# Streaming encoder step: a larger DMA count per gathered row in the planner, and fewer pauses in the row-tile normalization

## The chip, the cores and the metric

The kernel runs on one core of a Trainium2 chip. The metric is the device time of one execution in microseconds (us), from launch to end; lower is better. The engines named below are TensorE (PE, with its weight loads PEld), VectorE (DVE), ScalarE (ACT), GpSimd (POOL) and SyncE (SP), and the 16 DMA engines that all queues of the core share.

## What is computed

One layer of a hybrid encoder over 1024 prompt rows and 64 sample rows of width 1024: window attention and retention, an output projection and layer norm, then a mixture of 16,384 single-row experts (PEER) and a last layer norm. The step concerned is the mixture:

```python
def block(xb):                       # rows of the stream, after the first layer norm
    q = einsum('td,de->te', xb, wq).reshape(PEER_BLOCK, PEER_HEADS, 2, PEER_DK_HALF)
    s = einsum('tpcd,pcnd->tpcn', q, sub_keys)
    s1, i1 = top_k(s[:, :, 0], 16);  s2, i2 = top_k(s[:, :, 1], 16)
    # the best 16 of the 256 pairs, for each of 8 heads: 128 experts for each row
    top_s, sel = top_k(cand_s, 16);  eidx = take_along_axis(cand_i, sel, axis=-1)
    g = softmax(top_s)
    act = gelu(einsum('tpkd,td->tpk', u_tab[eidx], xb))
    return einsum('tpk,tpkd->td', g * act, v_tab[eidx])
h <- LN2(ALPHA * h + peer(h))
```

## The kernel before

The nine row tiles (eight of 128 prompt rows, one with the 64 sample rows, `TS`) go two ways through the mixture. Five tiles (`DENSE`, 640 rows) are **dense**: all 16,384 experts are multiplied with all rows, and a table `G` of gate weights, zero where an expert was not chosen, selects. The other four tiles are **gathered**: for each chosen expert its row of `u` and of `v` is fetched from DRAM by index. Both run at the same time, in what is called the dense stretch here.

**Dense work.** The experts are 128 blocks of 128. For block i, `u_mm` (L1352) multiplies the block's `u` with the 640 rows (48 matmuls into PSUM tile `pA`: high and low halves of the operands in three products), ACT applies the gelu, and DVE multiplies with the gate table (`ge<-pA,gt`, one such instruction for each block, so that it counts blocks). `v_mm` (L1392) multiplies the result with the block's `v`, for three blocks together: 10 units of 9 matmuls (`y`), each followed on DVE by an add into the sum in SBUF (`Y<-y,Y`). Three blocks with their 10 units are called a triple below. For each block SP issues loads of `u` (`ur<-ut`, 512 KB), of `v` (`vr<-vt`, twice 256 KB), and for each second block of five pieces of the gate table (`gt<-G`, 128 KB each); POOL makes the low halves (`ul`, `vl`, `wl`).

**Gathered work.** It comes in 448 slots, 64 for the sample tile (whose second half lies on partitions 64 to 127) and 128 for each of the tiles 5, 6 and 7. A slot needs one gather on POOL's queue (L239: 128 rows of `u` and `v` together, 8 KB each, into one of four buffers `uv`), then on DVE `uv<-uv,ph` (the dot product with the row), on ACT the gelu and gate (`gav`), and on DVE `pacc<-uv,gav,pacc` (the weighted add into PSUM tile `pacc`), which frees the buffer. Up to three gathers are issued ahead of their slot (`LEAD`).

**What sets the order.** Each engine runs its instructions in the order in which the program writes them. The dense units are written one by one, and after each of them `pump` (L392) decides whether slots are written next. It goes by a planner, `est`: counts of the time that each engine and the DMA have been given so far. For each gather `issue` (L232) adds a count to the planner's DMA time (L243) and from it notes when the data should be there (`avail`); `pump` writes no slot whose `avail` lies ahead of the planner's present time (the later of PE's and DVE's counts). So a larger count puts the slots farther apart among the dense units. The planner does not know what the chip does; it only sets an order.

**End of a gathered tile.** After its last slot the sum is copied to `gacc`, and `finish` (L271) normalizes it. For the first three of the four tiles the norm's weights `ln2_g` and `ln2_b` are loaded into one of the four `uv` buffers (`lnx`), so that three are left for gathers until the norm has read them. For the sample tile its second half is moved down to partitions 0 to 63 and added first. `finish` and `norm_out` (L289) are generators: each `yield` lets one further slot be written before the next step.

Of the kernel before, what the change touches and what calls it, by code (L numbers as in the profile page):

```python
# [135 lines left out]
def hymba_peer_step(ctx, tc, a, o):  # L136
    nc0 = tc.nc
    est = Est()
# [14 lines left out]
    def rows_bcast(ap, n):  # L153
        return bass.AP(tensor=ap.tensor, offset=ap.offset, ap=[[0, 128], [1, n]])
# [51 lines left out]
    def halves(t):  # L206
        return [t[:, 0:512], t[:, 512:1024]]
# [7 lines left out]
    def open_tile(t):  # L215
        d = spill[t]
        h1 = gat.tile([128, D], F32, name="gh1")
        g = gat.tile([128, 128], F32, name="gg", bufs=2)
        idx = gat.tile([128, 128], I32, name="gi", bufs=2)
        if t == TS:  # L220
            for i, (lo, hi) in enumerate(((0, NS), (NS, 128))):
                nc.sync.dma_start(h1[lo:hi], d["h1"])
                nc.sync.dma_start(g[lo:hi, 0:64], d["g"][:, i * 64:(i + 1) * 64])
                nc.sync.dma_start(idx[lo:hi, 0:64], d["idx"][:, i * 64:(i + 1) * 64])
        else:
            nc.sync.dma_start(idx, d["idx"])
            nc.sync.dma_start(h1, d["h1"])
            nc.sync.dma_start(g, d["g"])
        av = gat.tile([128, 128], F32, name="gav", bufs=2)
        tl[t] = dict(h1=h1, g=g, idx=idx, av=av, left=64 if t == TS else 128)  # L230

    def issue():  # L232
        k = ctl["issued"]
        t, j = slots[k]
        if t not in tl:
            open_tile(t)
        R = ctl["uvp"].tile([128, 2 * D], F32, name="uv", tag="uv")
        rows_uv[k] = R
        nc0.gpsimd.indirect_dma_start(out=R, out_offset=None, in_=a["uv"],  # L239
                                      in_offset=bass.IndirectOffsetOnAxis(ap=tl[t]["idx"][:, j:j + 1], axis=0))  # L240
        est.t["pool"] += 1.04
        ctl["pq"] = max(ctl["pq"], now()) + GTC
        est.t["dma"] = max(est.t["dma"], max(est.t["pe"], est.t["dve"]) - 3.0) + 2.6  # L243
        ctl["avail"][k] = max(est.t["dma"] + 2.0, max(ctl["pq"], now()) + ctl["slack"])
        ctl["issued"] = k + 1

# [10 lines left out]
    def accum(k):  # L257
        t, j = slots[k]
        d = tl[t]
        acc = banked(t, d, "acc")  # L260
        nc.vector.scalar_tensor_tensor(acc, rows_uv[k][:, D:2 * D], d["av"][:, j:j + 1], acc,
                                       op0=OP.mult, op1=OP.add)
        del rows_uv[k]
        ctl["done"] = k
        d["left"] -= 1
        if d["left"] == 0:
            d["acc"] = gat.tile([128, D], F32, name="gacc")
            nc.scalar.activation(d["acc"], acc, AF.Copy)
            ctl["fin"].append(finish(t, d))

    def finish(t, d):  # L271
        r, q = d["acc"], 128
        ln2, late = ctl["ln2"], t == TS
        if ln2 is None or t == TS:
            x = ctl["uvp"].tile([128, 2 * D], F32, name="lnx", tag="uv")
            ln2 = [x[:, 0:D], x[:, D:2 * D]]
            nc.sync.dma_start(ln2[0], rows_bcast(a["ln2_g"], D))
            if t == TS:
                q = NS
                nc.sync.dma_start(ln2[1][0:NS], r[NS:128])  # L280
                yield
                yield
                yield
                yield
                nc.vector.tensor_tensor(r[0:NS], r[0:NS], ln2[1][0:NS], op=OP.add)
            nc.sync.dma_start(ln2[1], rows_bcast(a["ln2_b"], D))
        yield from norm_out(gat, t, r, q, ln2)

    def norm_out(pool, t, r, q, ln2, st=None):  # L289
        wide = st is not None  # L290
        if not wide:
            st = pool.tile([128, 2, 6], F32, name="stf", bufs=2)
            for i, x in enumerate(halves(r)):
                nc.vector.bn_stats(st[:q, i], x[:q])
        mv = pool.tile([128, 3], F32, name="mvf", bufs=2)
        nc.vector.bn_aggr(mv[:q, 0:2], st[:q])
        nc.vector.tensor_scalar(mv[:q, 1:2], mv[:q, 1:2], EPS, None, op0=OP.add)
        nc.gpsimd.tensor_tensor(mv[:q, 2:3], mv[:q, 1:2], epsc[:q, 0:1], op=OP.pow)
        if wide:
            nc.gpsimd.tensor_tensor(mv[:q, 0:1], mv[:q, 0:1], mv[:q, 2:3], op=OP.mult)  # L300
            nc.gpsimd.tensor_scalar(mv[:q, 0:1], mv[:q, 0:1], -1.0, None, op0=OP.mult)
            yield
            nc.scalar.activation(r[:q], r[:q], AF.Identity, bias=mv[:q, 0:1], scale=mv[:q, 2:3])
            yield
            nc.gpsimd.tensor_tensor(r[:q], r[:q], ln2[0][:q], op=OP.mult)
            yield
            eng = nc.gpsimd if DENSE.index(t) in PAD else nc.vector
            eng.tensor_tensor(r[:q], r[:q], ln2[1][:q], op=OP.add)
            nc.sync.dma_start(o["y_p"][t * 128:(t + 1) * 128, :], r)
            return  # L310
        for _ in range(4):
            yield
        nc.vector.scalar_tensor_tensor(r[:q], r[:q], mv[:q, 0:1], ln2[0][:q], op0=OP.subtract, op1=OP.mult)
        yield
        nc.vector.scalar_tensor_tensor(r[:q], r[:q], mv[:q, 2:3], ln2[1][:q], op0=OP.mult, op1=OP.add)
        if t == TS:
            nc.sync.dma_start(o["y_s"], r[:q])
        else:
            nc.sync.dma_start(o["y_p"][t * 128:(t + 1) * 128, :], r)
# [5 lines left out]
    def prefetch():  # L325
        if ctl["uvp"] is None:
            return
        while (ctl["issued"] < len(slots) and ctl["issued"] < ctl["k"] + ctl["lead"]
               and ready[slots[ctl["issued"]][0]]):
            issue()  # L330
# [30 lines left out]
    def now():  # L361
        return max(est.t["pe"], est.t["dve"])
# [875 lines left out]
    def dense(hx):  # L1238
# [206 lines left out]
        for n, (kind, i) in enumerate(ops):  # L1445
            last = kind == "v" and i[0] == NG - 1
            ctl["most"] = 4
            if n == SL[1]:
                ctl["slack"] = SL[2]
            if 2 <= n < 2 + NT:  # L1450
                nc.sync.dma_start(Y[:, n - 2], spill[DENSE[n - 2]]["h1"])
            if kind == "u":
                if i % 2 == 0:
                    g_load(i // 2 + 1)
                yield from u_mm(i)
            else:
                yield from v_mm(*i)
                if n == len(ops) - 2 * NT - 1:
                    ctl["ln2"] = [vp.tile([128, NT * 256], F32, name="ln2r", tag="gt", bufs=2)[:, 0:D] for _ in range(2)]
                    for x, k in zip(ctl["ln2"], ("ln2_g", "ln2_b")):  # L1460
                        nc.sync.dma_start(x, rows_bcast(a[k], D))
            if last:
                if can_slot():
                    slot()
                for g in outs:
                    next(g, None)
                if i[1]:
                    outs.append(norm_out(xp, DENSE[i[2]], Y[:, i[2]], 128, ctl["ln2"], yst[i[2]]))
            yield
# [136 lines left out]
```

## Time and profile before

| what | value |
|---|---|
| median of 3 runs | 3320.02 us (3319.77 to 3331.34) |
| the profiled execution, its own time | 3355.53 us |
| span of that execution, first to last instruction | 3353.8 us |
| dense stretch while gathers run (1291.9 to 3140.3 us) | 1848.4 us, 113 blocks, 447 slots |
| rest of the dense blocks (3140.3 to 3297.7 us) | 157.4 us, 11 blocks, no slot but the last one's end |
| from there to the end of the span | 56.1 us |

Times in the rows count from the first instruction. The profile is one execution; DMA share is the mean busy share of the 16 DMA engines, the clock is TensorE's granted clock as a part of full speed. An engine's idle time is put down to what ended it.

### The profile page before, as it was taken

Reading aid. Unit: us, or ns where it says so; the run is one execution under the profiler, and the core shown is the slowest. Engines: PE = TensorE matmul, PEld = TensorE weight load, DVE = VectorE, ACT = ScalarE, POOL = GpSimd, SP = SyncE. Lnnn points to the kernel's source line nnn. Section 1 sums busy time; section 2 is a strip of 40 time slices with the busy share of each in tenths; the row PEclk is TensorE's granted clock in tenths of the full one; section 3 lists DMA queues with packets and bytes.
Section 4 is the critical chain, followed back from the end, with each engine's and each line's share of the span. In section 5 each row is a group of like instructions: output and inputs, shape, how many; then the busy total and the mean of one; then the engine's idle time right before and its main releaser. Section 6 shows DMA issues by size and latency. Waiting matters only on the chain.

```text
span 3353.8 us, 43782 instructions
## 1 busy us (share of the span) xinstructions
PE 2904.7 (87%) x15212; PEld 2495.5 (74%) x15212; DVE 2265.5 (68%) x5539; ACT 1115.8 (33%) x2599; POOL 1781.7 (53%) x1326
## 2 busy tenths in 40 slices
PE   4999889898996568888899988989899899989996
PEld 3777767677775557777788877878788788878895
DVE  1436976738639964776777777777778677877424
ACT  2332232332424663333333333333333333333221
POOL 0000155676663555665666666666666566666544
PEclk8999899899897789999999999999999999999998
DMA  6435235436432468898999989899989899999531
GB/s 178 145 112 213 82 84 145 95 62 167 97 79 79 114 181 325 326 346 304 349 355 354 350 336 340 321 347 341 355 323 361 318 349 349 351 367 340 199 98 63
DMA packets 296470, 813.19 MB, mean 242 GB/s; under 512 B 58296, under 2 KB 164520, under 8 KB 229176
## 3 DMA queue, kind: packets, MB, share of 16 engines
q0 software_dynamic: 97792, 469.94, 39.3%
q1 hardware_dynamic: 198024, 340.12, 29.9%
q8 instruction: 120, 1.97, 0.2%
q14 instruction: 102, 0.84, 0.1%
q10 hardware_dynamic: 432, 0.33, 0.0%
HBM read 753.04 MB, written 56.97 MB: 242 GB/s over the span
## 4 chain that ended last, share of the span: by engine, by line
PE 39%; DVE 22%; DMA 13%; issue 11%; POOL 10%; ACT 3%; SPq 1%; POOLq 0%; DVEq 0%; ACTq 0%
PE pA L108 13%; PE y L108 10%; DMA uv<-uv,gi 9%; PE pv L108 4%; PE pq L108 4%; DVE VI L108 4%; PE pa L108 3%; POOL uv L239 3%; POOL vl L108 3%; DVE pacc L108 3%; DVE ge L108 2%; DVE ob L108 2%; POOL ul L108 2%; POOL wl L108 2%; DVE oh L108 2%
## 5 line engine op out<-in xcount | busy, mean ns | idle before, releaser
L239 POOL DMA_INDIRECT uv<-uv,gi x448 | 432.1, 965 | 619.8 <-DVE pacc L108 561.2
L373 POOL DMA_INDIRECT G<-sg,si x256 | 382.3, 1493 | 620.2 <-DVE si L108 383.3
L108 DVE SCALAR_TENSOR_TENSOR uv<-uv,ph 128x1024 f32<-128x1024 f32 x448 | 544.1, 1215 | 238.1 <-DMA uv<-uv,gi 234.0
L108 PE MATMUL y<-vh,wh 128*128 128x512 f32 x1280 | 530.7, 415 | 185.1 <-DVE Y L108 182.9
L108 DVE SCALAR_TENSOR_TENSOR pacc<-uv,gav,pacc 128x1024 f32<-128x1024 f32 x448 | 575.6, 1285 | 2.2 <-ACT pacc L108 2.1
L108 PE MATMUL y<-vl,wh 128*128 128x512 f32 x1280 | 521.7, 408 | 2.0 <-POOL vl L108 2.0
L108 PE MATMUL y<-vh,wl 128*128 128x512 f32 x1280 | 520.8, 407 | 0.0
L108 PEld LDWEIGHTS y<-vh,wh 128*128 128x128 f32 x1280 | 250.8, 196 | 270.8 <-DVE Y L108 173.6
L108 DVE TENSOR_TENSOR Y<-y,Y 128x512 f32<-128x512 f32 x420 | 280.6, 685 | 178.8 <-PE y L108 175.1
L108 POOL TENSOR_TENSOR vl<-vr,vh 128x512 fp32r<-128x512 f32 x256 | 327.9, 1294 | 100.5 <-ACT vh L108 49.9
L108 PEld LDWEIGHTS pA<-xhi,uh 128*128 128x128 f32 x2048 | 331.5, 199 | 37.1 <-DVE ge L108 24.1
L108 PE MATMUL pA<-xhi,uh 128*128 128x320 f32 x2048 | 338.6, 320 | 23.3 <-DVE ge L108 23.3
L108 ACT ACTIVATE gav<-gav 128x1 f32<-128x1 f32 x448 | 88.7, 198 | 706.5 <-DVE uv L108 693.7
L108 PE MATMUL pA<-xlo,uh 128*128 128x320 f32 x2048 | 321.7, 309 | 0.0
L108 PE MATMUL pA<-xhi,ul 128*128 128x320 f32 x2048 | 321.2, 309 | 0.0
L108 POOL TENSOR_TENSOR ul<-ur,uh 128x1024 fp32r<-128x1024 f32 x128 | 309.6, 2418 | 4.8 <-ACT uh L108 2.5
L108 PEld LDWEIGHTS pA<-xlo,uh 128*128 128x128 f32 x2048 | 306.5, 188 | 0.0
L108 PEld LDWEIGHTS pA<-xhi,ul 128*128 128x128 f32 x2048 | 305.6, 187 | 0.0
L108 PEld LDWEIGHTS y<-vh,wl 128*128 128x128 f32 x1280 | 252.9, 198 | 57.0
L108 PEld LDWEIGHTS y<-vl,wh 128*128 128x128 f32 x1280 | 252.5, 197 | 48.9 <-POOL vl L108 2.9
L108 ACT ACTIVATE pA<-pA 128x640 f32<-128x640 f32 x128 | 88.0, 688 | 511.9 <-PE pA L108 505.9
L108 DVE TENSOR_TENSOR ge<-pA,gt 128x640 f32<-128x640 f32 x128 | 105.2, 822 | 212.0 <-ACT pA L108 145.3
(287 smaller groups left out, 4385.4 us busy)
## 6 DMA issues: line engine op xcount, KB each, us to landing
ur<-ut SPq DMA_DIRECT2D x128, 512.0 KB
vr<-vt SPq DMA_DIRECT2D x256, 256.0 KB
gt<-G SPq DMA_DIRECT2D x320, 128.0 KB
w<-w_r SPq DMA_DIRECT2D x32, 1024.0 KB
G<-gs SPq DMA_DIRECT2D x24, 1024.0 KB
G<-zeros SPq DMA_DIRECT2D x16, 1024.0 KB
w<-w_out SPq DMA_DIRECT2D x16, 1024.0 KB
w<-w_pq SPq DMA_DIRECT2D x16, 1024.0 KB
```

The lines of the kernel that those rows point to most:

```text
L108: return f(*a, **k)
L239: nc0.gpsimd.indirect_dma_start(out=R, out_offset=None, in_=a["uv"], in_offset=bass.IndirectOffsetOnAxis(ap=tl[t]["idx"][:, j:j + 1], axis=0))
L373: nc0.gpsimd.indirect_dma_start(out=spill[t]["G"], out_offset=bass.IndirectOffsetOnAxis(ap=idx[:, j:j + 1], axis=0), in_=g[:, j:j + 1], in ...
```

## The change

Two things. The planner's count of DMA time for one gather goes from 2.6 to 2.85. And fewer slots are written between the steps of a gathered tile's normalization: two fewer before the sample tile's halves are added, and three fewer (one instead of four) between a tile's statistics and the first of its two normalizing instructions. No instruction is added or taken away on any engine.

```diff
@@ issue (L243)
-        est.t["dma"] = max(est.t["dma"], max(est.t["pe"], est.t["dve"]) - 3.0) + 2.6
+        est.t["dma"] = max(est.t["dma"], max(est.t["pe"], est.t["dve"]) - 3.0) + 2.85
@@ finish
                 yield
                 yield
-                yield
-                yield
                 nc.vector.tensor_tensor(r[0:NS], r[0:NS], ln2[1][0:NS], op=OP.add)
@@ norm_out
-        for _ in range(4):
-            yield
+        yield
         nc.vector.scalar_tensor_tensor(r[:q], r[:q], mv[:q, 0:1], ln2[0][:q], op0=OP.subtract, op1=OP.mult)
```

PE's order is the same, and so is everything ahead of the first gather. DVE, ACT, POOL and SP get the same instructions in another order. Before, the first 446 adds of slots stand between the 4th and the 117th `ge` (113 blocks, four in most of them, 3.95 in the mean), and after the change between the 4th and the 127th (123 blocks, mostly 3, 4, 4 in turn, 3.63 in the mean). The next add follows in the block behind, and the add of slot 448 comes in both after all dense work.

On DVE near the end of the dense stretch, before, with the last slot that stands among dense blocks (`ge`, `Y` are dense; `uv,gav` and `pacc` are a slot):

```order
L108 TENSOR_TENSOR ge<-pA,gt 128x640
L108 TENSOR_TENSOR Y<-y,Y 128x512 x2
L108 SCALAR_TENSOR_TENSOR uv,gav<-uv,ph_21198 128x1024
L108 SCALAR_TENSOR_TENSOR pacc<-uv,gav,pacc 128x1024
L108 TENSOR_TENSOR Y<-y,Y 128x512 x2
L108 TENSOR_TENSOR ge<-pA,gt 128x640
L108 TENSOR_TENSOR Y<-y,Y 128x512 x3
```

Behind these rows follow ten more blocks without a slot. And on DVE after the change, around the last such slot:

```order
L108 SCALAR_TENSOR_TENSOR uv,gav<-uv,ph_22081 128x1024
L108 SCALAR_TENSOR_TENSOR pacc<-uv,gav,pacc 128x1024
L108 TENSOR_TENSOR Y<-y,Y 128x512
L108 SCALAR_TENSOR_TENSOR uv,gav<-uv,ph_22081 128x1024
L108 SCALAR_TENSOR_TENSOR pacc<-uv,gav,pacc 128x1024
L108 TENSOR_TENSOR Y<-y,Y 128x512 x2
L108 TENSOR_TENSOR ge<-pA,gt 128x640
L108 TENSOR_TENSOR Y<-y,Y 128x512 x6
L108 BN_STATS yst_26947<-Y 128x6
```

The slots now reach up to the last block; what follows the last `ge` on DVE is the same in both.

On POOL at the same place, before, with the last gather (`uv<-uv,gi`) between the making of low halves (`ul`, `vl`, `wl`):

```order
L239 DMA uv<-uv,gi 128x2048
L108 TENSOR_TENSOR ul<-ur,uh 128x1024
L239 DMA uv<-uv,gi 128x2048
L108 TENSOR_TENSOR vl<-vr,vh 128x512
L108 TENSOR_TENSOR wl<-ge,wh 128x640
L108 TENSOR_TENSOR vl<-vr,vh 128x512 x2
```

And on POOL after the change:

```order
L108 TENSOR_TENSOR vl<-vr,vh 128x512 x2
L239 DMA uv<-uv,gi 128x2048 x2
L108 TENSOR_TENSOR ul<-ur,uh 128x1024
L239 DMA uv<-uv,gi 128x2048 x2
L108 TENSOR_TENSOR wl<-ge,wh 128x640
L108 TENSOR_TENSOR vl<-vr,vh 128x512 x3
L108 TENSOR_TENSOR wl<-ge,wh 128x640
```

The last gathers stand just ahead of the last two `wl`, where before the low halves of some ten blocks followed them.

On DVE at the end of tile 5, the first of three alike tiles, before; the statistics (`stf`, `mvf`) stand eight rows ahead of the first row here, with one slot between:

```order
L108 SCALAR_TENSOR_TENSOR pacc<-uv,gav,pacc 128x1024
L108 TENSOR_TENSOR Y<-y,Y 128x512 x2
L108 SCALAR_TENSOR_TENSOR uv,gav<-uv,ph_16750 128x1024
L108 SCALAR_TENSOR_TENSOR pacc<-uv,gav,pacc 128x1024
L108 TENSOR_TENSOR ge<-pA,gt 128x640
L108 SCALAR_TENSOR_TENSOR uv,gav<-uv,ph_16750 128x1024
L108 SCALAR_TENSOR_TENSOR pacc<-uv,gav,pacc 128x1024
L108 SCALAR_TENSOR_TENSOR gacc<-gacc,mvf,lnx 128x1024
L108 TENSOR_TENSOR Y<-y,Y 128x512 x2
L108 SCALAR_TENSOR_TENSOR uv,gav<-uv,ph_16750 128x1024
L108 SCALAR_TENSOR_TENSOR pacc<-uv,gav,pacc 128x1024
L108 SCALAR_TENSOR_TENSOR gacc<-gacc,mvf,lnx 128x1024
```

And on DVE after the change, from the statistics on:

```order
L108 BN_STATS stf<-gacc 128x6 x2
L108 BN_AGGR mvf<-stf 128x2
L108 TENSOR_SCALAR mvf<-mvf 128x1
L108 TENSOR_TENSOR Y<-y,Y 128x512 x3
L108 SCALAR_TENSOR_TENSOR uv,gav<-uv,ph_17235 128x1024
L108 SCALAR_TENSOR_TENSOR pacc<-uv,gav,pacc 128x1024
L108 SCALAR_TENSOR_TENSOR gacc<-gacc,mvf,lnx 128x1024
L108 SCALAR_TENSOR_TENSOR uv,gav<-uv,ph_17235 128x1024
L108 SCALAR_TENSOR_TENSOR pacc<-uv,gav,pacc 128x1024
L108 SCALAR_TENSOR_TENSOR gacc<-gacc,mvf,lnx 128x1024
```

One slot instead of four stands between the statistics and the first instruction that reads `lnx`.

## Rows read from the trace of the kernel before

**Rows 1.** The page: span, and DMA share in 40 slices, in tenths.

```profile
span 3353.8 us, 43782 instructions
...
DMA  6435235436432468898999989899989899999531
```

**Rows 2.** Windows with and without slots: busy of PE, PEld, DVE, ACT, POOL; clock, DMA share, GB/s.

```profile
1291.90:3140.30 1848.40, 1662.40 (x8821) 1478.08 (x8819) 1392.01 (x1849) 602.64 (x1468) 1163.11 (x900) 0.95 0.92 341
3140.30:3297.70 157.40, 156.31 (x867) 142.35 (x868) 38.16 (x54) 37.65 (x57) 69.60 (x44) 0.99 0.27 87
```

**Rows 3.** Waits of 1291.9 to 3140.3 us: who for whom, us in total, times, longest.

```profile
POOL uv L239 <- DVE pacc L108: 561.2, 266, 8.0
...
DVE uv L108 <- DMA uv<-uv,gi: 234.0, 112, 5.2
PE y L108 <- DVE Y L108: 180.8, 86, 8.7
```

**Rows 4.** The chain that ended last, its last 300 us: start, us, what.

```profile
3098.32 9.61 DMA uv<-uv,gi
...
3129.43 8.12 DMA uv<-uv,gi
...
3147.38 7.04 PE pA L108 x48
...
3160.56 7.04 PE pA L108 x48
...
3272.17 7.04 PE pA L108 x48
```

**Rows 5.** Windows of a triple each, pacc instructions alone (x: slots); clock, DMA share, GB/s.

```profile
1672.95:1718.27 45.32, 15.41 (x12) 1.00 0.99 376
...
2456.00:2508.37 52.37, 15.41 (x12) 0.90 0.86 312
2508.37:2554.90 46.53, 15.41 (x12) 1.00 0.99 372
...
2929.13:2975.75 46.62, 15.41 (x12) 1.00 0.99 374
...
3027.47:3075.54 48.07, 15.42 (x12) 1.00 0.99 371
sum 1156.44, DVE 371.28; mean DVE 15.47
```

**Rows 6.** DMA: the gathers' queue (packets, MB, share), and issues by tile.

```profile
q0 software_dynamic: 97792, 469.94, 39.3%
...
ur<-ut SPq DMA_DIRECT2D x128, 512.0 KB
vr<-vt SPq DMA_DIRECT2D x256, 256.0 KB
gt<-G SPq DMA_DIRECT2D x320, 128.0 KB
```

**Rows 7.** Timeline of SP at the end of tile 5.

```profile
2092.45 0.33 SPq L85 DMA_DIRECT2D lnx<-ln_g  x1
2093.12 0.33 SPq L85 DMA_DIRECT2D lnx<-ln_b  x1
```

**Rows 8.** Timeline of DVE there, from the statistics to the norm's second instruction.

```profile
2093.52 1.29 DVE L108 BATCH_NORM_STATS2 stf<-gacc 128x6 f32<-128x512 f32 x2 [1.09 <-ACT gacc L108]
...
2116.64 1.28 DVE L108 SCALAR_TENSOR_TENSOR gacc<-gacc,mvf,lnx 128x1024 f32<-128x1024 f32 x1
...
2121.37 1.33 DVE L108 SCALAR_TENSOR_TENSOR gacc<-gacc,mvf,lnx 128x1024 f32<-128x1024 f32 x1
```

**Rows 9.** Window of all engines at the same place.

```profile
2105.00:2120.00 15.00, 13.28 (x74) 11.89 (x75) 9.46 (x12) 3.78 (x9) 7.78 (x5) 1.00 0.46 159
```

**Rows 10.** Timeline of DVE at the last two dense blocks.

```profile
3280.09 0.82 DVE L108 TENSOR_TENSOR ge<-pA,gt 128x640 f32<-128x640 f32 x1 [7.18 <-ACT pA L108]
...
3297.36 0.82 DVE L108 TENSOR_TENSOR ge<-pA,gt 128x640 f32<-128x640 f32 x1 [7.20 <-ACT pA L108]
```

## The prediction

> **What bounds the kernel now.** I first read the page's DMA slices: between 1291.9 us, where the slots begin, and 3140.3 us the 16 DMA engines are busy at nine tenths in nearly every slice, and then the share drops to a third and less while the dense work goes on [rows 1]. The windows of the two parts say what that costs. In the first, 113 blocks take 1848.4 us, 16.36 us each, with PE busy 1662.4 us of it, DMA at 0.92 and 341 GB/s. In the second, 11 blocks take 157.4 us with PE busy 156.3 us, DMA at 0.27 and 87 GB/s [rows 2]. So PE is the bound at the end, and in the nine tenths before it something else is. The regular pace of PE alone is read from the chain: nine blocks between the `pA` pieces at 3147.38 and 3272.17 us, 124.8 us, 13.87 us a block or 41.6 us a triple [rows 4].
>
> The waits name the path in the first part. DVE sat idle 234.0 us for gathered rows, and PE sat idle 180.8 us for DVE's `Y` adds, which stand behind those slots in DVE's order [rows 3]. POOL waited 561.2 us for DVE to free a gather buffer [rows 3]; POOL's own work has room, but a gather issued late is a gather that lands late.
>
> **Is it bandwidth or latency?** The gathers move 469.94 MB in 448 slots, 1.049 MB each; `u`, `v` and gate table are 67.1 + 67.1 + 41.9 = 176.1 MB in 128 blocks, 1.376 MB a block [rows 6]. For 446 slots and 113 blocks that makes 467.9 + 155.5 = 623.4 MB; 341 GB/s over 1848.4 us are 630.3 MB, 1.1% more (tile loads), so the bytes are accounted for. I cut 24 triples away from the ends of gathered tiles: 1156.44 us, 48.19 us each, with 371.28 us of adds at 1.285 us, 289 slots, 12.04 a triple [rows 5]. Four of them run at a DMA share of 0.99 and 371 to 376 GB/s (mean 373), others at 312 [rows 5]. So there is a ceiling near 373 GB/s, and the mean is nine tenths of it: phases in which DVE waits for data alternate with phases in which it waits for PE and frees no buffer.
>
> **Spreading the slots.** The order shows that 446 slots go into 123 blocks instead of 113, 41 triples with 10.88 slots each. No byte and no instruction is saved; ten blocks that ran at a DMA share of 0.27 take a part of the load. The sum is made for the stretch from 1291.9 to 3297.7 us, 2005.8 us now [rows 2].
>
> First way, the rate stays: 467.9 + 123 x 1.376 = 637.2 MB, with the 1.1% 644 MB, at 341 GB/s 1889 us. Then comes the last block, 17.3 us between the last two `ge` [rows 10], and the last two groups' longer blocks, 1.5 us (157.4 - 17.3 = 140.1 us for ten, against 138.7). That is 1908 us, a gain of 98 us.
>
> Second way, the rate sinks, since PE comes nearer. At the ceiling a triple of before needs 12.04 x 1.049 + 4.13 = 16.76 MB / 373 = 44.9 us and takes 48.19, so 3.3 us are lost to the two alternating waits, where data lie 3.3 us above PE's 41.6. After, 15.54 MB / 373 are 41.7 us, level with PE: both waits are then equally likely, and the loss should grow. I put it at half as much again, 4.9 us (an estimate; it can't be read before), so 46.6 us a triple, 1911 us for 41. The ends of three gathered tiles come on top: now 1848.4 - 37.67 x 48.19 = 33 us, after 25 (next part). With 18.8 us for the end, 1955 us, a gain of 51 us. If the loss stays at 3.3 us, a triple takes 45.0 and the gain is 117 us.
>
> I take the middle of 98 and 51 us, 75 us, since I have no row that favours one; 51 and 117 stay as ends.
>
> The Trainium skill ("DMA: Bandwidth & Descriptors", Specifications) gives about 358 GB/s as the HBM limit of a core. Four triples here ran above it, at 371 to 376 [rows 5], so the measurement decides. By the page a triple after the change would need 15.54 MB / 358 = 43.4 us, above PE's 41.6: DMA would stay the bound, the rate would hold, and the gain would be nearer the 98 us.
>
> **Shorter normalization.** At the end of tile 5 the norm's weights are issued into a gather buffer at 2092.45 us, and the second norm instruction reads them at 2121.37 [rows 7, 8]. For 30 us only three buffers carry gathers, and in 2105 to 2120 us the DMA share is down to 0.46, 159 GB/s [rows 9]. Three slots fewer at 1848.4 / 446 = 4.1 us free the buffer 12 us sooner; in proportion that is 13 of the 33 us lost at the three tiles. Against it, the first norm instruction now comes one slot after the statistics. From the issue that is 1.1 us to the statistics, 1.3 us for their main part [rows 7, 8], three `Y` adds at PE's pace for a unit ((41.6 - 3 x 7.04) / 10, some 2.05 us [rows 4]) and a slot whose add alone is 1.3 us: some 10 us. Landings of gathers in the full stretch took 8.1 and 9.6 us [rows 4]. DVE thus waits for nothing or for 2 us, three times; what it holds up is the next slots and `Y` adds in its own order, and through these PE. I take a gain of 8 us, which the 25 us above contain; the ends are -6 and +13. For the sample tile the moved half has two slots, 8 us, to land, which is tight too; it lies within these ends.
>
> **The end.** Behind the last `ge` DVE's order is the same, so the 56.1 us from there are kept. New is that the last gathers stand ahead of the last two `wl` on POOL, and slots ahead of the last `Y` adds on DVE. A late gather, 8 to 10 us [rows 4], could hold PE's last units once; between 0 and 10 us. I take 0, because the pace above already holds such waits.
>
> **The sum.** The profiled execution took 3355.53 us, of which 1.7 us lie outside its span [rows 1]; it is 35.5 us above the median of 3320.02, so I take the difference of 75 us and not the ratio: 3245 us.
>
> **Rivals.** *Every slot costs its wait wherever it stands.* A triple is 48.19 - 41.6 = 6.6 us above PE's pace for 12.04 slots, 0.55 us a slot. If that is a price of the slot itself (DVE's time for it in the path of the `Y` adds, the buffer's way round), 447 slots cost the same anywhere, and only the norm's 8 us are won: 3312 us, no change. For it: PE's waits are on DVE, not on DMA [rows 3]. Against it: DVE is busy only 1392 of 1848 us [rows 2], and idles 234 us for data.
>
> *The pace of a triple stays, and more triples run at it: slower.* If a gather's way round (issue, landing, DVE's place for it, buffer free) sets the pace, 41 triples at 48.19 us, 33 us and 18.8 us make 2028 us, 22 us more than now: 3342 us. It decides from the pace: (2005.8 - 33 - 18.8) / 41 = 47.6 us a triple is break-even, 1.2% below today's. For it: POOL's 561 us of waiting for buffers, with four of them. Against it: DMA shares of 0.99 with twelve slots in 45 to 48 us, which a fixed way round would not allow.
>
> The Trainium skill (the same page, "Anatomy of one DMA — SWDGE (gpsimd) path") fits a fixed 2.0 us plus bytes / 436e3 to one such DMA, 4.4 us for a gather. The chain shows 8.1 and 9.6 us [rows 4], so by that rule half of the landing is queueing behind other transfers, which shrinks as the load is spread; had the landings been 4.4 us, this rival would have had more.
>
> *The rate rises to the ceiling* and PE takes over nearly everywhere: beyond the 117 us, under 3200 us. It wants no loss from alternation, of which every slice shows some.
>
> **How the numbers follow.** The forecast with gains of 40 to 120 us gets 0.63, a smaller gain of 17 to 40 us (loss per triple of more than 5.5 us) 0.12, the beyond-ceiling case 0.04, the slot-price rival 0.13, the slower one 0.08. A change of 0.5%, 17 us, is about what a measurement of this kernel can tell from none. So faster has 0.63 + 0.12 + 0.04 = 0.79, same 0.13, slower 0.08. The range goes from a gain of 120 us to one of 5 us, 3200 to 3315: it takes in the slot-price rival's 3312 us and about half of its chance, and leaves out the slower case (0.08), the other half (0.06) and the extreme (0.04), 0.18 together.
>
> **What would show it.** Right: DMA share of 0.88 to 0.95 up to the last block, no stretch at 0.27; triples of 45.0 to 46.6 us; DVE's wait for gathers well under 234 us and PE's for `Y` under 180.8; gathers issued up to some 10 us before the last `ge`. The norm: less than 30 us from `lnx` load to last read, with no DMA wait over 2 us on DVE there. Wrong: triples still near 48 us (the pace rival), or near 47.6 with DVE's wait for data down and its wait for PE up by as much (the slot price); DVE waiting on `lnx`; a late gather that leaves PE idle in the last two blocks.

## The result, and the profile after

The changed kernel takes 3217.5 us in the median (3210.46 to 3224.04), the kernel before 3323.6 in the same comparison: ratio 0.9674, 95% interval 0.9652 to 0.9696, some 106 us less. The forecast was 3245 us, 75 us less, in a range of 3200 to 3315.

One warning for reading the rows. The profiled execution of before (3355.53 us) lies 32 us above the median, that of the changed kernel (3212.71 us) 5 us below its own. Traces of the two differ by 143 us, of which 106 are the change. An experiment below, the one with only the shorter normalization, keeps before's slots and was profiled within 3 us of its median; its rows stand here for "slots as before" where sizes matter.

The page after: span, PE, DMA share and GB/s in 40 slices, to be held against [rows 1].

```profile
span 3210.9 us, 43762 instructions
...
PE   4999889899897566999999999899999999999995
...
DMA  6434325445433448899999999899999999999982
GB/s 169 166 119 186 113 68 143 104 97 132 99 72 71 134 120 261 330 353 349 357 361 350 366 358 341 321 349 349 347 351 347 340 354 348 344 345 341 344 330 102
```

The stretch at a DMA share of 0.27 is gone; nine tenths now reach up to the last dense block. Windows of the same kind as [rows 2], from the 4th `ge` to the 127th and on to the last (busy of PE, PEld, DVE, ACT, POOL; clock, DMA share, GB/s), then the whole:

```profile
1283.70:3137.20 1853.50, 1756.43 (x9604) 1574.77 (x9603) 1421.62 (x1887) 633.31 (x1514) 1228.81 (x940) 0.98 0.93 346
3137.20:3154.80 17.60, 16.29 (x86) 13.74 (x85) 10.86 (x16) 4.26 (x11) 6.23 (x5) 1.00 0.40 132
...
1283.70:3154.80 1871.10, 1772.72 (x9688) 1588.52 (x9687) 1432.48 (x1902) 637.57 (x1525) 1235.04 (x944) 0.98 0.93 344
```

123 blocks take 15.07 us each; before, 113 blocks took 16.36 in the profile shown and 16.10 in the one nearer the median. The waits in the first of these windows, to be held against [rows 3]:

```profile
POOL uv L239 <- DVE pacc L108: 453.8, 257, 7.3
...
DVE uv L108 <- DMA uv<-uv,gi: 132.5, 83, 5.2
...
PE y L108 <- DVE Y L108: 91.9, 66, 5.6
```

DVE's wait for gathered rows fell from 234.0 to 132.5 us, PE's wait for `Y` adds from 180.8 to 91.9 (in the profile nearer the median they were 211.1 and 163.2). Triples away from the ends of gathered tiles, `pacc` instructions alone, as [rows 5] (27 triples; DVE's 380.02 us are 296 slots):

```profile
1701.51:1745.63 44.12, 14.11 (x11) 1.00 0.99 372
1745.63:1787.17 41.54, 14.12 (x11) 1.00 0.95 358
...
2918.80:2967.24 48.44, 14.12 (x11) 0.93 0.88 330
...
sum 1220.53, DVE 380.02; mean DVE 14.07
```

A triple takes 45.2 us in the mean, where it took 48.19 [rows 5]; the quickest shown took 41.5, PE's own 41.6. At the end of tile 5 the first load of the norm's weights and their two readers (SP, then DVE, as [rows 7, 8]):

```profile
2075.59 0.33 SPq L85 DMA_DIRECT2D lnx<-ln_g  x1
```

```profile
2085.91 1.28 DVE L108 SCALAR_TENSOR_TENSOR gacc<-gacc,mvf,lnx 128x1024 f32<-128x1024 f32 x1
...
2089.44 3.38 DVE L108 SCALAR_TENSOR_TENSOR gacc<-gacc,mvf,lnx 128x1024 f32<-128x1024 f32 x1
```

The buffer is held 17 us instead of 30, and no idle time stands before either reader. The second reader took 3.38 us where it took 1.33 before [rows 8]; the profile shows no cause for these 2 us.

### The profile page after: what moved, and what is told of

Same layout as the page of the kernel before. It is cut to its first block, busy times and chain, and to the rows that moved or that the text cites. A ratio compares the mean times of both kernels' runs of the same rounds, so it can differ in the third digit from the quotient of the medians.

```text
span 3210.9 us, 43762 instructions
## 1 busy us (share of the span) xinstructions
PE 2848.3 (89%) x15212; PEld 2455.0 (76%) x15212; DVE 2270.1 (71%) x5539; ACT 1113.0 (35%) x2599; POOL 1784.1 (56%) x1326
## 4 chain that ended last, share of the span: by engine, by line
PE 40%; DVE 24%; DMA 12%; issue 11%; POOL 9%; ACT 3%; SPq 1%; POOLq 0%; DVEq 0%; ACTq 0%
PE pA L108 14%; PE y L108 10%; DMA uv<-uv,gi 6%; PE pv L108 5%; PE pq L108 5%; DVE pacc L108 3%; PE pa L108 3%; POOL uv L239 3%; DVE VI L108 3%; POOL vl L108 3%; DVE ge L108 2%; DVE ob L108 2%; DVE prd L108 2%; DMA vr<-vt 2%; POOL ul L108 2%
## 5 line engine op out<-in xcount | busy, mean ns | idle before, releaser
L108 DVE SCALAR_TENSOR_TENSOR uv<-uv,ph 128x1024 f32<-128x1024 f32 x448 | 543.3, 1213 | 135.3 <-DMA uv<-uv,gi 132.5
L108 PE MATMUL y<-vh,wh 128*128 128x512 f32 x1280 | 514.7, 402 | 98.2 <-DVE Y L108 93.2
L108 PE MATMUL y<-vl,wh 128*128 128x512 f32 x1280 | 507.9, 397 | 0.2 <-POOL vl L108 0.2
L108 PE MATMUL y<-vh,wl 128*128 128x512 f32 x1280 | 507.4, 396 | 0.0
L108 PEld LDWEIGHTS y<-vh,wh 128*128 128x128 f32 x1280 | 243.6, 190 | 177.1 <-DVE Y L108 95.6
L108 PE MATMUL pA<-xhi,uh 128*128 128x320 f32 x2048 | 331.0, 315 | 23.8 <-DVE ge L108 23.8
L108 PEld LDWEIGHTS pA<-xhi,uh 128*128 128x128 f32 x2048 | 321.6, 194 | 36.0 <-DVE ge L108 24.6
L108 PEld LDWEIGHTS y<-vh,wl 128*128 128x128 f32 x1280 | 244.6, 191 | 53.8
L108 PEld LDWEIGHTS y<-vl,wh 128*128 128x128 f32 x1280 | 244.3, 191 | 44.8 <-POOL vl L108 0.6
L108 POOL TENSOR_TENSOR wl<-ge,wh 128x640 fp32r<-128x640 f32 x128 | 201.2, 1572 | 65.6 <-ACT wh L108 65.2
```

The costliest lines, as they stand in the source:

```text
L108: return f(*a, **k)
```

## The experiments

All ratios are to the kernel before on the same chip. Theory A was that DMA bytes set the pace; B that a slot costs its wait wherever it stands; C that a gather's way round has a fixed latency. Theory L came up after the first eight runs.

**The two parts apart.** The count alone (2.85, long pauses):

```diff
-        est.t["dma"] = max(est.t["dma"], max(est.t["pe"], est.t["dve"]) - 3.0) + 2.6
+        est.t["dma"] = max(est.t["dma"], max(est.t["pe"], est.t["dve"]) - 3.0) + 2.85
```

> The planner's count alone goes to 2.85; the normalization keeps its four (and four more) pauses. Theory A (bandwidth: the same bytes spread over ten more blocks): it gives most of the change's 106 us, 80 to 95 us, so 3228 to 3243 us, and DMA share stays at 0.9 up to the last block. Theory B (each slot costs its wait wherever it stands, the gain came from the buffer freed sooner): no change, 3315 to 3330 us.

Measured 3232.3 us, ratio 0.9704 (0.9655 to 0.9752), 92 us less. And the pauses alone (count 2.6):

```diff
-                yield
-                yield
                 nc.vector.tensor_tensor(r[0:NS], r[0:NS], ln2[1][0:NS], op=OP.add)
@@
-        for _ in range(4):
-            yield
+        yield
```

> The shorter pauses of the normalization alone, with the count 2.6 and so the slots where they stood. Theory A: the nine blocks at the end of each of three gathered tiles, 152 us each in the profile of before, come down by 5 to 7 us each, 15 to 20 us together: 3303 to 3309 us. Theory B: most of the 106 us, under 3250 us. If DVE waited for the norm's weights as the prediction feared: 0 to 6 us slower than before.

Measured 3314.4 us, ratio 0.9965 (0.9944 to 0.9986), 10 us less, somewhat under A's 15 to 20. The parts add up within their intervals: 92 + 10 of 106. B, which gave the norm all of it, falls. The trace of the second run gives before's slots a second look (113 blocks, then 11 without slots):

```profile
1284.57:3103.70 1819.13, 1652.19 (x8821) 1469.21 (x8819) 1392.10 (x1849) 602.33 (x1468) 1162.63 (x900) 0.96 0.93 347
3103.70:3259.60 155.90, 154.80 (x868) 141.24 (x869) 38.11 (x54) 37.66 (x57) 69.66 (x44) 1.00 0.27 90
sum 1975.03, PE 1806.99 PEld 1610.45 DVE 1430.21 ACT 640.00 POOL 1232.29; mean PE 903.50 PEld 805.23 DVE 715.11 ACT 320.00 POOL 616.15
```

**Half the spread.**

```diff
-        est.t["dma"] = max(est.t["dma"], max(est.t["pe"], est.t["dve"]) - 3.0) + 2.85
+        est.t["dma"] = max(est.t["dma"], max(est.t["pe"], est.t["dve"]) - 3.0) + 2.72
```

> The changed kernel with the count at 2.72: the last slot among dense blocks stands behind block 122 instead of 117 (before) or 127 (changed). Theory A, time goes by the blocks over which the bytes are spread: half of the count's gain, so with the norm's 55 to 65 us under before: 3258 to 3268 us, triples at 46.5 to 47 us. Theory B: within 10 us of the changed kernel, 3210 to 3225 us, as the norm is the same.

Measured 3231.8 us, ratio 0.9717 (0.967 to 0.9764), 26 us below A's range and a little above B's. Five of the ten blocks of spread gave 83 of the 97 us that lie between the shorter pauses alone and the changed kernel (83 give or take 16, by the interval). The 118 blocks with slots run at 15.25 us, with a higher rate than either neighbour:

```profile
1283.60:3083.20 1799.60, 1686.69 (x9202) 1504.62 (x9201) 1406.16 (x1871) 616.72 (x1494) 1197.86 (x920) 0.98 0.94 354
3083.20:3170.60 87.40, 87.40 (x488) 79.52 (x487) 22.46 (x32) 20.06 (x32) 37.54 (x24) 1.00 0.27 85
```

A block there carries 3.2% fewer bytes (5.34 MB, not 5.52) and takes 5.3% less time than with the shorter pauses alone. A fixed rate can't do that; something else was in the way at 2.6. The waits of the two stretches, first with the shorter pauses alone, then with 2.72:

```profile
DVE uv L108 <- DMA uv<-uv,gi: 211.1, 122, 5.4
PE y L108 <- DVE Y L108: 163.2, 91, 8.7
```

```profile
DVE uv L108 <- DMA uv<-uv,gi: 196.1, 132, 4.2
...
PE y L108 <- DVE Y L108: 109.4, 94, 8.2
```

DVE waits for gathers nearly as long as before, in more and shorter pieces, and much less of it reaches PE. So the sum of DVE's waits does not measure what they cost.

**Beyond the end.**

```diff
-        est.t["dma"] = max(est.t["dma"], max(est.t["pe"], est.t["dve"]) - 3.0) + 2.85
+        est.t["dma"] = max(est.t["dma"], max(est.t["pe"], est.t["dve"]) - 3.0) + 3.1
```

> The changed kernel with the count at 3.1: 407 slots stand in the dense blocks (3.3 a block), 40 are left for after the last block. Theory A: the blocks get faster, to 14.3 to 14.6 us (PE alone 13.87), 55 to 85 us less than in the changed kernel, and the 40 slots behind them take 2.8 to 3.1 us each, 112 to 125 us, with PE idle: 3245 to 3285 us, slower than the changed kernel. Theory C (a gather's way round sets the pace, with four buffers): the slots after the end take about as long as the slots in the stretch, over 4 us each, 160 us and more: over 3290 us.

Measured 3217.8 us, ratio 0.9666 (0.962 to 0.9713), the same as the changed kernel and below A's range and C's. The windows of the 123 blocks, and of what follows the last `ge`:

```profile
1286.03:3066.55 1780.52, 1730.75 (x9595) 1557.71 (x9594) 1336.69 (x1779) 611.96 (x1444) 1197.15 (x904) 1.00 0.92 340
3085.20:3221.00 135.80, 27.88 (x98) 18.64 (x96) 107.57 (x148) 26.53 (x79) 61.46 (x60) 0.63 0.77 277
```

The blocks came down to 14.48 us as expected, 73 us for the stretch. Of the 40 slots left over, 35 stand behind the last `ge`, and what follows it takes 80 us longer (135.8 against 56.1), not 112 to 125: a part of the slots runs beside the closing normalization of the dense tiles, where the changed kernel keeps DVE busy for 29.6 of 56.1 us and the DMA share is 0.17. So the two sides nearly cancel, and 2.85 is no sharp optimum.

**Fewer bytes, same order.** Each fourth tile of the gate table is loaded and used for eight blocks, so the dense sum is of other gates; 0.246 MB a block less:

```diff
-            if i < 64:
+            if i < 64 and i % 4:
+                for _ in DENSE:
+                    est.t["dma"] += 128 * 256 * 4 / 405e3
+                gq[i] = ctl["gt"]
+            elif i < 64:
@@
-                gq[i] = gt
+                gq[i] = ctl["gt"] = gt
```

> The kernel before, every order as it was, but only each fourth tile of the gate table is loaded and used for eight blocks (so the dense sum is of other gates): 0.246 MB a block less, 4.5% of the 5.52 MB, and no work less on any compute engine. Theory A (DMA bytes set the pace where slots stand): 4.5% or more of 16.1 to 16.4 us a block, 80 to 110 us over 113 blocks: 3215 to 3245 us. Theory B (each slot costs its wait whatever the bytes) and theory C (a gather's fixed way round): within 15 us of before, 3308 to 3338 us.

Measured 3268.1 us, ratio 0.9832 (0.9812 to 0.9853): 59 us less, where A wanted 80 to 110 and B and C none. The same in the changed kernel:

> The same cut of 0.246 MB a block in the changed kernel, from 5.18 to 4.94 MB; orders as in the changed kernel, other gates in the dense sum. Theory A: data are still part of the bound, and the pace goes toward that of the count 3.1 (4.85 MB a block, 14.48 us): 15.07 to some 14.55 us, 60 us less, 3145 to 3170 us. If the changed kernel is bound by PE alone: no more than 15 us less, over 3200 us. Theory B: no change.

Measured 3188.7 us, ratio 0.9597 (0.9571 to 0.9623): 29 us under the changed kernel (26 by the ratios), half of what A wanted and twice what PE alone would allow. So bytes count in both kernels, but 4.5% fewer bytes bought some 3.2% of a block's time in before's order (59 us over 113 blocks, 0.52 us of some 16.2). In the changed kernel the same bytes bought 0.27 us a block (15.07 to 14.80). They are not all of it.

**Half the gather, same order.** A gather fetches the row of `u` alone, and the add takes it in place of `v` (other values in the gathered tiles):

```diff
-        nc0.gpsimd.indirect_dma_start(out=R, out_offset=None, in_=a["uv"],
+        nc0.gpsimd.indirect_dma_start(out=R[:, 0:D], out_offset=None, in_=a["u1"],
@@
-        nc.vector.scalar_tensor_tensor(acc, rows_uv[k][:, D:2 * D], d["av"][:, j:j + 1], acc,
+        nc.vector.scalar_tensor_tensor(acc, rows_uv[k][:, 0:D], d["av"][:, j:j + 1], acc,
```

> The kernel before, every order as it was, but a gather fetches the row of u alone (0.524 MB instead of 1.049) and the weighted add takes it in place of v: the same gathers, slots and DVE instructions, half their bytes (other values in the gathered tiles). 3.45 MB a block is 10 us at 345 GB/s, far under PE's 13.87. Theory A: the blocks with slots come down to 14.0 to 14.4 us, 190 to 240 us less, 3085 to 3135 us. Theory B (DVE's time for a slot in the path): 3300 us or more. Theory C (way round of fixed latency): 3280 us or more.

Measured 3175.9 us, ratio 0.9554 (0.9532 to 0.9576), 151 us less. And in the changed kernel:

> The same halved gathers in the changed kernel. Theory A: the spreading is worth nothing once bytes don't bind; blocks at 14.0 to 14.3 us in both, so within 15 us of the halved gathers in the kernel before: 3070 to 3130 us. If the spreading helped for another reason (fewer slots beside each Y add, less contention on DVE or POOL), it stays 50 us or more under the other.

Measured 3156.7 us, ratio 0.9497 (0.9477 to 0.9516). The two now differ by 19 us, of which the norm makes some 10 if it is worth as much here as it was alone. Without the weight of the gathers the spreading is then worth some 9 us instead of 92, which was what A wanted to see (within 15 us); B and C, which saw little or no gain from halved gathers, fall as the main cause. But A wanted 190 to 240 us from the first. And the runs don't tell a byte from the time it takes: halved gathers also land sooner (below). The window of the 113 blocks with slots of the first of these runs says what is left:

```profile
1284.22:2959.39 1675.17, 1599.88 (x8813) 1434.52 (x8812) 1386.96 (x1849) 600.62 (x1468) 1164.94 (x900) 0.99 0.73 237
```

14.82 us a block, 0.95 us above PE's 13.87, at a DMA share of 0.73. That is 0.24 us a slot which the DMA's rate does not explain.

**The lead.** One size of the orders moves with the count and is not a number of bytes: how much work of PE is written between a gather and the dot product that needs it. In matmul columns at 13.87 us a block, mean over slots 11 to 400, it is 6.0 us at 2.6, 7.2 at 2.72, 8.1 at 2.85 and 9.4 at 3.1. From issue to dot product the traces show 9.2, 9.0, 9.5 and 10.0 us, but this holds the waits of the engines too, and the time that a row lies in its buffer. How long a gather takes to land is read from its own line: with the shorter pauses alone (2.6), with the count alone (2.85), and with halved gathers in the changed kernel:

```profile
DMA to landing us min/median/max: 5.3/7.9/12.1
```

```profile
DMA to landing us min/median/max: 5.3/7.8/11.3
```

```profile
DMA to landing us min/median/max: 4.0/5.0/8.7
```

So at 2.6 a gather was asked for some 2 us too late if PE were not to wait, and from 2.85 on no more in the middle of the spread, though the slowest landings still come late; halved, 5.0 us fit into the lead of 6.0. This is theory L. A fifth gather buffer makes the lead longer and keeps the spacing: in the written order the slots stand earlier by some 6 us of PE's work in the mean, at the same spacing (3.5 us of that work to a slot in both orders), and no byte is spread. It fits only if `v` gives up buffers, and that alone was measured first, in the changed kernel:

```diff
-NVS, NWB = 6, 6
+NVS, NWB = 5, 6
@@
-                v = vp.tile([128, 512], F32, name="vr", bufs=5)
+                v = vp.tile([128, 512], F32, name="vr", bufs=3)
```

> The changed kernel with fewer buffers for v (three instead of five for the loaded tile, five instead of six for its halves), which makes room for the next two. It measures that cut alone; loads of v run ahead less, and ACT may wait once a triple for a half: within 12 us of the changed kernel by all theories, 3210 to 3232 us.

Measured 3330.7 us, ratio 1.0001 (0.9979 to 1.0022): all theories missed, since the cut itself costs 113 us. Its waits, and SP's, show where:

```profile
ACT uh L108 <- DMA ur<-ut: 184.3, 42, 8.7
...
DVE uv L108 <- DMA uv<-uv,gi: 124.5, 93, 3.9
```

```profile
SPq L85 <- POOL vl L108: 1447.5, 227, 15.2
```

ACT now waits for the load of `u`, 184.3 us in 42 places, where it waited 3.6 us once in the changed kernel. SP issues all loads in order; a load of `v` that waits for its buffer holds up the load of `u` behind it. For POOL's `vl`, which frees a buffer of `v`, SP waits 1447.5 us between 1290 and 3100 us, and 816.6 in the changed kernel. With this as the base, the fifth buffer in the kernel before and in the changed one (both with the cut):

```diff
-NB, LEAD = 4, 3
+NB, LEAD = 5, 4
```

> The kernel before (count 2.6, slots as close as they were, no byte less in a block, long pauses) with a fifth gather buffer and gathers issued up to four ahead, at the price of the same cut in v's buffers. In the written order a gather then stands 9.1 us of PE's own work ahead of its dot product, instead of 6.0 before and 8.1 in the changed kernel; from issue to dot product the traces show 9.2 to 9.5 us. Theory L (the lead sets the wait: a gather is issued too late, and wider spacing made the lead longer): most of the count's 92 us comes without any spreading, 3225 to 3250 us. Theory A (bytes over the rate): no byte is spread, so 0 to 30 us less, 3295 to 3330 us.

Measured 3261.4 us, ratio 0.9806 (0.9783 to 0.983): 70 us under before, in spite of the cut (what the cut costs in before's order was not measured), and 11 us above L's range. Its 113 blocks, and their wait for gathers:

```profile
1292.27:3046.88 1754.61, 1626.17 (x8806) 1449.25 (x8807) 1390.67 (x1852) 595.30 (x1470) 1168.40 (x900) 0.97 0.95 359
```

```profile
ACT uh L108 <- DMA ur<-ut: 229.2, 48, 14.9
...
DVE uv L108 <- DMA uv<-uv,gi: 14.1, 9, 4.8
```

> The changed kernel with the fifth buffer: the lead in the written order goes from 8.1 to 11.7 us of PE's work, slots and bytes stay where they are. Theory L: DVE's wait for gathers falls from 132 us to under 70, and the time by 25 to 50 us: 3170 to 3195 us. Theory A: 5.18 MB a block already move at 346 GB/s; toward the ceiling of 373 there are some 15 us to win at most, 3203 to 3220 us.

Measured 3251.9 us, ratio 0.9785 (0.9755 to 0.9815): 79 us under its base, though not under the changed kernel, and above the ranges of both theories, which had left out the cut. With the fifth buffer DVE's wait for gathers is 14.1 us in before's order, with no byte spread, instead of 211.1 (pauses alone) or 234.0 [rows 3], and a single wait of 1.2 us in the changed order, instead of 124.5 in its base; and the rate rises to 359 GB/s without any spreading. L holds for that wait. What took its place in the time is the wait for `u`, which is the cut's. How fast a fifth buffer without the cut would be was not tried, so the 70 and 79 us are not the worth of a longer lead alone.

**The rest of a slot.** Halved gathers (with the two edits above) in eight buffers of half the size, two of which take the norm's weights, up to seven ahead; the main lines:

```diff
-NB, LEAD = 4, 3
+NB, LEAD = 8, 7
@@
-        R = ctl["uvp"].tile([128, 2 * D], F32, name="uv", tag="uv")
+        R = ctl["uvp"].tile([128, D], F32, name="uv", tag="uv")
```

> Halved gathers as before in the kernel before (only the row of u, taken for v too), in eight half-size buffers and up to seven ahead, so that neither bytes nor lead should bind; slots as close as before. It measures what a slot costs by itself. If the 0.95 us a block that halved gathers kept above PE's own 13.87 us was lead: down to 14.0 to 14.3 us, 60 to 95 us under the 3176 us of the halved gathers in four buffers, 3080 to 3115 us. If it is DVE's time for a slot beside the Y adds: within 20 us of 3176.

Measured 3163.3 us, ratio 0.9509 (0.9492 to 0.9527), 13 us under the halved gathers in four buffers. The window of its 113 blocks, and PE's wait:

```profile
1283.81:2942.47 1658.66, 1594.76 (x8809) 1432.94 (x8808) 1394.27 (x1852) 601.50 (x1470) 1164.88 (x895) 0.99 0.74 238
```

```profile
PE y L108 <- DVE Y L108: 62.5, 65, 5.3
```

So most of the 0.95 us a block is not lead. A block still takes 14.68 us with no wait for gathers in sight, and PE waits for `Y` adds 62.5 us: what is left fits DVE's time for a slot ahead of an add, a small part of B, but no run here took only that away.

## Why the prediction was right, and where its size was off

**What bounds the kernel.** Right: where slots stand, data set the pace; where they don't, PE. The halved gathers show it from the other side. "Data" is more than the rate of bytes, though: the prediction noted that a gather issued late lands late, and gave it no term.

**The pace of a triple.** This is the term that was mis-sized. The prediction's first way (the rate stays) gave 98 us, its second (the loss from alternating waits grows by half, 46.6 us a triple) 51, and it took the middle, 67 us for the spread and 8 for the norm. Measured: 92 for the count, and triples of 45.2 us, 3.5 us above the 41.7 that 373 GB/s would allow, where 3.3 were lost before. The loss hardly grew; with 45.2 us the prediction's own sum gives a gain of 109 us. The step that failed is the estimate of half as much again: it took the alternation as a matter of chance between two equal sides. Half the spread bringing 83 of 97 us, and DVE's wait for gathers gone with a fifth buffer, fit a gather that was issued too late; wider spacing lengthens the lead as well as thinning the bytes.

The first way came closer, and partly by luck. With the 347 GB/s of the profile nearer the median it gives some 1875 us for the stretch, and 1871.1 were measured. But the rate did not stay: it was 354 GB/s at half the spread, 346 at 2.85 and 340 at 3.1.

How the 92 us divide can be estimated only. The gate table gave 0.52 us a block for 0.246 MB in before's order and 0.27 in the changed one. Spreading takes 0.34 MB off a block, so 0.37 to 0.71 us by these two slopes, of the 1.03 us by which the block got shorter (16.10 to 15.07, both with the short pauses). So between a third and two thirds go by bytes, and the rest by lead or by what no run set apart. The two are not separate quantities, since fewer bytes also land sooner; this stays open.

The prediction also wanted the queueing in a gather's landing to shrink as the load is spread. It did not: the median landing was 7.9 us with the slots as before and 7.8 with the count alone.

**Shorter normalization.** 8 us forecast, 10 measured (5 to 19 by the interval). The feared wait for the weights did not come in the changed kernel: 10.3 us from issue to the first reader at tile 5, no idle time before it. With the pauses alone it came once, for 1.4 us.

**The end.** Right: 56.1 us behind the last `ge` in both. A late gather did hold DVE once, for 2.52 us just ahead of the last but one `ge`, and PE only briefly, 0.69 and 0.59 us.

**The rivals.** The slot's own price is at most some 0.2 us and not 0.55, and it stays with the slot: the spread's gain didn't need it. The slower case, an unchanged triple, fell with 45.2 against its break-even of 47.6; what spoke for it, the wait for buffers, was a true sign of gathers issued too late, which the wider spacing helped instead of leaving it as it was. The case beyond 117 us did not come either, though the profiles alone, at 143, would have suggested it.

## What to carry to other kernels

When a planner places fetched work among a bound engine's work, compare two numbers: how much of that engine's work is written between a fetch and its use (6.0 us here), and how long the fetch takes from issue to landing in the trace (7.9 us). Issue to use is the wrong number: it grows with the lead. Where the first is the smaller, spacing the fetches, or one more buffer, may win more than the bytes say, as half the spread did here. Spread such work up to the end of the stretch; beyond it, what fits beside an idle tail cost little here, so the optimum was flat. And be careful with taking buffers from a load that shares an in-order queue with others: here the queue stopped at the load that waited, which cost 113 us.

## What the runs showed of the hardware that was not expected

**PE's own time shrank with its waits.** The same matmuls (some 9,690 recorded) of the stretch were busy 1807.0 us with the pauses alone and 1772.7 in the changed kernel, at a granted clock of 0.96 and 0.98; with the count 3.1, at 1.00, it was less again. Of 104 us between these two stretches (1975.0 and 1871.1), 34 are PE's busy time and 70 its idle time (168.0 to 98.4). The prediction had no term for the first. Two windows of the kernel before show a low clock behind an idle PE, and two `y` matmuls in each their pace:

```profile
2080.00:2085.00 5.00, 0.84 (x4) 0.38 (x2) 5.00 (x8) 3.27 (x8) 2.71 (x3) 0.93 0.78 292
2085.00:2090.00 5.00, 4.85 (x13) 4.02 (x14) 3.63 (x6) 1.75 (x4) 4.80 (x5) 0.50 1.04 401
```

```profile
2080.00 0.39 PE L108 MATMUL y<-vh,wh 128*128 128x512 f32 x1
2080.23 0.39 PE L108 MATMUL y<-vl,wh 128*128 128x512 f32 x1
...
2085.74 0.63 PE L108 MATMUL y<-vl,wh 128*128 128x512 f32 x1
2086.17 0.63 PE L108 MATMUL y<-vh,wl 128*128 128x512 f32 x1
```

PE was busy 0.84 us of the first five and then ran at 0.50, the lower level of 1.2 GHz: matmuls of one size start 0.43 us apart, where they started 0.23 us apart before. The Trainium skill ("TensorE: Matmul & The Clock Gate", Part 1) says that the array's clock has these two levels and drops when the array idles; the rows agree.

**Issue to use is not a gather's own time.** A gather of 1.049 MB landed 7.9 us after its issue in the median, one of half the bytes after 5.0 us, at a DMA share of 0.71. From issue to dot product it was 9.2 us in before's order and 8.1 with halved gathers there, but 11.9 us with the fifth buffer and 22.4 with halved gathers in eight buffers: a row that has landed lies in its buffer until its place on DVE comes.

**The sustained rate.** The highest mean over a whole stretch was 359 GB/s, with the fifth buffer, at a share of 0.95; single triples reached 376 [rows 5], and one of the 5 us windows above 401.
